# Two middle down projections as seven half-size products each, with scratch tiles divided anew, in a two-layer decoder step

## The chip, the cores and the metric

The kernel runs on one core of a Trainium2 chip, as one launch. The metric is the device time of the launch in microseconds (us), less is better. Engines: PE (TensorE) multiplies, ACT (ScalarE) and DVE (VectorE) work on tiles element by element, POOL (GpSimd) is used here for little but issuing DMAs, SP (SyncE) only issues DMAs.

## The reference

One inference step of a two-layer decoder in float32, for a prompt of 512 tokens and 8 single-token samples, with model width 1024 and feed-forward width 2816. Around each layer's token mixer stand two half layers, each a SwiGLU whose result is halved:

```python
def _swiglu(x, wg, wu, wd):
    return (jax.nn.silu(x @ wg) * (x @ wu)) @ wd
...
x = x + 0.5 * _swiglu(_rmsnorm(x, norm_g[l, 0]), ffn_w_gate[l, 0], ffn_w_up[l, 0], ffn_w_down[l, 0])
...  # pooling mixer in layer 0, sliding-window attention in layer 1
x = x + 0.5 * _swiglu(_rmsnorm(x, norm_g[l, 2]), ffn_w_gate[l, 1], ffn_w_up[l, 1], ffn_w_down[l, 1])
```

So there are four SwiGLUs, called here by `fi` = 0 to 3. They hold nearly all of the products.

## The kernel before

The residual stream lies transposed in SBUF, as eight tiles `x[k]` of 128 features by 520 tokens. Every operand of a product is split into a high and a low float32r part (`xh`/`xl`, `hh`/`hl` for activations, `wh`/`wl` for weights), and a product is three matrix products (`terms`): high by high, low by high, high by low. A matmul covers 128 rows, 128 columns and half of the tokens, 260.

**A half layer** (`ffn`) goes through its 22 blocks of 128 hidden features in three parts, `PARTS = (8, 8, 6)`. For each block a tile makes gate and up products over the eight feature tiles, SiLU and the product of both (`g`), and splits it (`hidden`). After each part its down projection adds into `x`: eight output blocks, each from two pieces of weights, every piece for both halves of the tokens (`mm`, L510 in the profile). The first `NPL[fi]` tiles of a half layer, (4, 3, 2, 3), are plain ones; the others are Strassen tiles (`strassen_tile`; their matmuls are L538): gate and up for both token halves and both halves of the features form a 2 x 2 block product, made from seven products (`product`, 12 matmuls each) instead of eight. For this the activations' sums T1 to T4 are made once per half layer (`sums`), and the weights' sums S1 to S4 for every tile.

**The weights** go through the class `Weights`. Two lists are written in advance: chunks (up to 1 MB, in a ring of three `raw` buffers) and pieces (128 x 512). `W.get` hands out the next piece; `W.prefetch` has `_split` work five pieces ahead: ACT copies the piece to `wh` (L233), DVE subtracts to get `wl` (L234), each in a ring of six. A Strassen chunk has seven pieces, in the order A11, S1, A22 of the chunk before, S2, A12, S4, S3; its own A22 comes after the next chunk's S1. S2 and S4 are made on DVE in the `raw` buffer (L198, L202). S1 and S3 are made by DMA: `loaded` loads the half block once more into a tile `S` (a ring of four), and POOL issues two adding DMAs, into `S` (L192) and into `raw` (L193). Two calls in `_split` set how far this runs ahead, after each piece:

```python
held = any(c < it[0] for c, _, _ in self.items[self.ns + 1 : self.ns + 3])
self.load(it[0] + self.ca - held)
self.add_up(it[0] + 1)
```

`load` issues chunks up to the given one (`ca` is 2), `add_up` calls `loaded` up to the given one. `held` is true where one of the next two pieces is of an earlier chunk.

**The order of the work.** The program is written in one order, and a scheduler in the framework then orders each engine's queue by its own estimates. What goes through `later` keeps the order in which it was written; all loads of weights do so (`ld`, L325, on SP). Each engine takes its queue in order, and so does SP: an issue that waits for a free buffer holds up the issues behind it. PSUM is used as four pairs of banks (`duo`); ACT copies partial results out of it (L618, L620, L623), DVE the rest (L626, L630, L635; in the down projection L688 and L689). Scratch tiles of a half layer come from a pool with two buffers a name, but the name `sb` has four (three in `fi` = 2) of a full tile's size and serves partial sums, the sums T1 to T4 and the down projection's `u`.

Of the kernel before, what the change touches and what calls it, by code (L numbers as in the profile page):

```python
# [11 lines left out]
F32 = mybir.dt.float32  # L12
# [6 lines left out]
P = 128  # L19
# [10 lines left out]

FIRST = 264
NPL = (4, 3, 2, 3)
HD = 64
NB = SP // P
WINS = (2, 4, 8, 16)
# [90 lines left out]
class Weights:  # L126
# [48 lines left out]
                c[2](c[1])  # L175
            self.na += 1

    def sums(self, ch, again):

        G, V, tmp = self.nc.gpsimd, self.nc.vector, {}

        def blk(raw, r, c):
            return rows(raw)[:, r - 1, 4 * c - 4 : 4 * c, :]

        def loaded(raw):
            s1 = self.splp.tile([P, 4, P], F32, tag="S", name="S", bufs=4)
            tmp[1] = s1  # L190
            again(s1)
            G.dma_start(s1, blk(raw, 2, 2), accum_op=ALU.add)  # L192
            G.dma_start(blk(raw, 2, 1), blk(raw, 1, 1), accum_op=ALU.add)  # L193

        self.chunks[ch][2] = loaded

        def s2(raw):
            V.tensor_tensor(blk(raw, 1, 1), blk(raw, 1, 1), tmp[1], op=ALU.add)  # L198
            return blk(raw, 1, 1)

        def s4(raw):
            V.tensor_tensor(blk(raw, 1, 2), blk(raw, 1, 2), blk(raw, 1, 1), op=ALU.add)  # L202
            return blk(raw, 1, 2)

        self.piece(ch, lambda raw: blk(raw, 1, 1))
        self.piece(ch, lambda raw: tmp[1])
        self.last()
        self.piece(ch, s2)
        self.piece(ch, lambda raw: blk(raw, 1, 2))
        self.piece(ch, s4)  # L210
        self.piece(ch, lambda raw: blk(raw, 2, 1))
        self.late = (ch, lambda raw: blk(raw, 2, 2))

    def _split(self, i):
        nc = self.nc
        while self.ns <= min(i, len(self.items) - 1):
            it = self.items[self.ns]
            self.load(it[0])
            self.add_up(it[0])
            src = it[1](self.chunks[it[0]][1])  # L220
            n = src.shape[1]
            if it[2] is not None:
                dh, dl = it[2]()
                wh = wl = None
            else:
                wh = self.splp.tile([P, 4, P], F32R, tag="wh", name="wh")
                wl = self.splp.tile([P, 4, P], F32R, tag="wl", name="wl")
                dh, dl = wh[:, :n, :], wl[:, :n, :]
            if len(src.shape) == 4:
                dh = dh.rearrange("p k (e d) -> p k e d", e=2)  # L230
                dl = dl.rearrange("p k (e d) -> p k e d", e=2)
            pin = self.pin if wh is not None else self.pin_home
            pin(nc.scalar.activation(dh, src, AF.Copy))  # L233
            pin(nc.vector.tensor_tensor(dl, src, dh.bitcast(F32), op=ALU.subtract))  # L234
            it[2] = (wh, wl)
            held = any(c < it[0] for c, _, _ in self.items[self.ns + 1 : self.ns + 3])
            self.load(it[0] + self.ca - held)
            self.add_up(it[0] + 1)
            self.ns += 1

    def get(self):
# [10 lines left out]
def yoco_step(ctx, tc, ins, outs):  # L252
# [21 lines left out]
    def pair(tags, shape, dtype=F32R):  # L274

        return tuple(big.tile(shape, dtype, tag=t, name=t) for t in tags)

    XX, TT, HH = ("xh", "xl"), ("th", "tl"), ("hh", "hl")

    def later(ins):  # L280

        return tc.keep_in_program_order(ins)

    ordered = [False]

    def seq(ins):

        return later(ins) if ordered[0] else ins

    def split(dst, src, scale=None):  # L290

        hi, lo = dst
        if scale is None:
            seq(S.activation(hi, src, AF.Copy))
            seq(V.tensor_tensor(lo, src, hi.bitcast(F32), op=ALU.subtract))
        else:
            seq(S.activation(hi, src, AF.Copy, scale=scale))
            seq(V.scalar_tensor_tensor(lo, src, scale, hi.bitcast(F32), op0=ALU.mult, op1=ALU.subtract))

    ordered = [False]  # L300

# [22 lines left out]
    def ld(dst, src):  # L324
        return lambda raw: later(nc.sync.dma_start(dst(raw), src))  # L325
# [22 lines left out]
    def plan_ffn(l, f):  # L348
        g3 = w_gate[l, f].rearrange("(k p) c -> p k c", p=P)
        u3 = w_up[l, f].rearrange("(k p) c -> p k c", p=P)  # L350
        d3 = w_down[l, f].rearrange("(k p) c -> p k c", p=P)
        t0 = 0
        for n in PARTS:
            for j in range(t0, t0 + n):
                c = slice(j * P, (j + 1) * P)
                cuts = ((0, 4), (4, 8)) if (l, f, j) == (0, 0, 0) else ((0, 8),)
                ch = W.chunk(
                    *[
                        ld(lambda raw, k=k, o=o: rows(raw)[:, o, k[0] : k[1], :], w3[:, k[0] : k[1], c])
                        for k in cuts  # L360
                        for o, w3 in ((0, g3), (1, u3))
                    ]
                )
                if j < NPL[2 * l + f]:
                    for k0 in (0, 4):
                        for o in (0, 1):
                            W.piece(ch, lambda raw, k0=k0, o=o: rows(raw)[:, o, k0 : k0 + 4, :])
                else:
                    W.sums(ch, ld(lambda t: t, u3[:, :4, c]))
            for c in range(4):  # L370
                ch = W.chunk(ld(lambda raw, n=n: raw[:, :n, :], d3[:, t0 : t0 + n, c * 256 : (c + 1) * 256]))
                if (l, f) == (1, 1) and t0 + n == sum(PARTS) and c > 1:
                    if c == 2:
                        plain(ch, n, 0)
                    for k in range(n):
                        W.home(ch, *last_piece(k, c))
                    continue
                plain(ch, n, 0)
                plain(ch, n, P)
            t0 += n  # L380
# [64 lines left out]
    def hcols(t, hf):  # L445
        return t[:, hf * H : (hf + 1) * H]
# [11 lines left out]
            order(V.tensor_tensor(acc[:, :TOK], acc[:, :TOK], sq, op=ALU.add))  # L458

    pss_ = [None]  # L460
    nsb = [4]

    def rstd_tok(tiles=(0, P, 2 * P, 3 * P, 400)):

# [80 lines left out]
                )  # L545

    def hidden(g, hs):
        hp = pair(hs.tags, [P, TOK])
        split(hp, g)
        hs.append(hp)  # L550

    class Hidden(list):


        def __init__(self, tags):
            self.tags = tags

    copied, there = [], [False]

# [46 lines left out]
    def strassen_tile(tmp, xx, tt, hs):  # L606
# [5 lines left out]
        g = tmp.tile([P, TOK], F32, tag="g", name="g")  # L612
        t = tmp.tile([P, TOK], F32, tag="t", name="t")
        sa = tmp.tile([P, TOK], F32, tag="sa", name="sa")
        sb = tmp.tile([P, H], F32, tag="sb", name="sb", bufs=nsb[0])
        a, c = duo()[:, 0, :], duo()
        product(B(xx, lo, 0), a)
        S.copy(hcols(sa, 0), a[:, :H])  # L618
# [18 lines left out]

        unfinished.append(rest)

    def sums(tmp, n, tt):  # L640


        for k in range(4):
            xa = tmp.tile([P, TOK], F32, tag="sa", name="xa")
            xb = tmp.tile([P, TOK], F32, tag="sa", name="xb")
            for kk, xn in ((k, xa), (k + 4, xb)):
                S.activation(xn, x[kk], AF.Copy, scale=gcol(n, kk))
            t12 = tmp.tile([P, TOK], F32, tag="sb", name="t12", bufs=nsb[0])
            t34 = tmp.tile([P, TOK], F32, tag="sb", name="t34", bufs=nsb[0])
            b11, b12, b21, b22 = hcols(xa, 0), hcols(xa, 1), hcols(xb, 0), hcols(xb, 1)  # L650
            t1, t2, t3, t4 = hcols(t12, 0), hcols(t12, 1), hcols(t34, 0), hcols(t34, 1)
            later(V.tensor_tensor(t1, b11, b12, op=ALU.subtract))
            V.scalar_tensor_tensor(t2, t1, -1.0, b22, op0=ALU.mult, op1=ALU.subtract)
            tt[k] = pair(TT, [P, TOK])
            split(tt[k], t12)
            yield
            later(V.tensor_tensor(t3, b22, b12, op=ALU.subtract))
            V.scalar_tensor_tensor(t4, t2, -1.0, b21, op0=ALU.mult, op1=ALU.subtract)
            tt[k + 4] = pair(TT, [P, TOK])
            split(tt[k + 4], t34)  # L660
            yield

    def ffn(fi, tmp, mov, hooks, tt, tags, after, before_last=None, first=None, by_parts=None, hold=False):

        j = 0
        for pi, n in enumerate(PARTS):
            last = pi == len(PARTS) - 1
            hs = Hidden(tags)
            for _ in range(n):
                if j == 0 and first is not None:  # L670
                    plain_end(tmp, *first, hs)
# [5 lines left out]
                    strassen_tile(tmp, mov, tt, hs)  # L677
                j += 1
                W.pin = lambda ins: ins
            nk = (n + 1) // 2  # L680
            rest = NH if last and by_parts is not None else 0

            def add(m, bank, hfs):
                c = slice(hfs[0] * H, (hfs[-1] + 1) * H)
                u = tmp.tile([P, TOK], F32, tag="sb", name="u", bufs=nsb[0])[:, c]
                parts = lambda z: z.rearrange("p (h c) -> p h c", c=H)
                pin = later if last and hold and m == KT - 1 else seq
                pin(V.tensor_tensor(parts(u), bank[:, hfs[0] : hfs[-1] + 1, :H], parts(R[:, c]), op=ALU.mult))  # L688
# [341 lines left out]
        V.tensor_tensor(out, out, sw, op=ALU.add)  # L1030

    mov4 = []
    nsb[0] = 3
    with ff_pool() as tmp:

        s4 = sinks.rearrange("p (g i b e) -> p g i b e", g=2, i=4, b=4)
# [97 lines left out]
        hooks = [step, outputs] + [step] * 4  # L1134
        ffn(2, tmp, mov3, hooks, tt, XX, deferred(4, tmp, "g", HH, mov4), attention_prep())

    nsb[0] = 4

    mov5, mov6 = [], []
    with tc.tile_pool(name="at", bufs=2) as at:  # L1140
# [346 lines left out]
    with ff_pool() as tmp:  # L1487
# [95 lines left out]
        def tail(hs):  # L1583
# [28 lines left out]

            def add(j, bank):
                m = KT - NH + j
                u = tmp.tile([P, TOK], F32, tag="sb", name="u", bufs=nsb[0])[:, c]
                seq(V.tensor_tensor(u, bank, R[:, c], op=ALU.mult))
                seq(V.scalar_tensor_tensor(x[m][:, c], u, -0.5, x[m][:, c], op0=ALU.mult, op1=ALU.add))
                sq = tmp.tile([P, TOK], F32, tag="g", name="sq")
# [110 lines left out]
```

## Time and profile before

| | |
|---|---|
| three runs | 1679.82, 1685.45, 1685.54 us; median 1685.45 us |
| span of the profiled execution, first to last instruction | 1678.4 us |
| PE busy | 1655.2 us (99%) |
| DVE busy | 1241.2 us (74%) |
| ACT busy | 890.0 us (53%) |
| POOL busy | 165.6 us (10%) |
| DMA | 225.97 MB moved, mean 135 GB/s |

The page gives the span of the profiled execution and no total for it; the three runs are 1.4 to 7.1 us longer than that span. Times in the rows below are us from the span's start. A row of a timeline has start, duration, engine, line, operation, output and input, and in brackets how long the engine was idle before and what ended it. SPq is SP issuing a DMA. In the rows of a tile, "DMA to landing" is the time from a DMA's issue to its data being in place.

### The profile page before, as it was taken

To read this page: it belongs to the slowest core of one execution; us is meant where nothing else is said; L and a number is where in the kernel's file an instruction comes from. 1 tells how busy PE (TensorE), PEld (TensorE's weight loads), DVE (VectorE), ACT (ScalarE), POOL (GpSimd) and SP (SyncE) were. 2 spreads that over 40 slices of the span, in tenths; PEclk is the share of its full clock that TensorE was granted. 3 is DMA by queue.
4 is the path that set the end of the run, shared out by engine and by line. 5 is a ranking of instruction groups with operands and counts; after the bars stand their busy time and mean duration, and the time that the engine had idled before them with its cause. 6 is when DMAs were issued, how large, how long until landed. Compare 5 with 4: busy or idle time off the path is not lost.

```text
span 1678.4 us, 34457 instructions
## 1 busy us (share of the span) xinstructions
PE 1655.2 (99%) x13770; PEld 1645.5 (98%) x13770; DVE 1241.2 (74%) x2361; ACT 890.0 (53%) x1768; POOL 165.6 (10%) x224
## 2 busy tenths in 40 slices
PE   9999999999999999999999999999989999999997
PEld 9999999999999999999999999999989999999997
DVE  6866866887975875878775875886787785785776
ACT  5743643666652652655552652655785653463455
POOL 0101101000101101100201101101210100110100
PEclk9999999999999999999999999999999999999999
DMA  8646846652655745643755755653222554674641
GB/s 215 137 122 136 174 140 137 176 161 73 144 145 133 176 145 133 151 132 94 170 148 132 171 151 133 151 149 86 70 51 76 133 136 130 147 173 133 143 127 52
DMA packets 314541, 225.97 MB, mean 135 GB/s; under 512 B 9726, under 2 KB 290022, under 8 KB 314340
## 3 DMA queue, kind: packets, MB, share of 16 engines
q1 hardware_dynamic: 287614, 177.86, 37.6%
q0 software_dynamic: 23008, 40.83, 14.8%
q10 hardware_dynamic: 3758, 5.09, 1.0%
q8 instruction: 108, 1.77, 0.4%
q14 instruction: 53, 0.43, 0.1%
HBM read 180.30 MB, written 5.04 MB: 110 GB/s over the span
## 4 chain that ended last, share of the span: by engine, by line
PE 94%; ACT 2%; DVE 2%; issue 1%; DMA 0%; POOL 0%; ACTq 0%; DVEq 0%; POOLq 0%
PE ps L538 46%; PE ps L510 43%; PE ps L917 1%; PE ps L942 1%; ACT sm L1256 1%; PE ps L1312 1%; ACT xh L310 0%; PE ps L1281 0%; PE ps L1603 0%; PE ps L1610 0%; PE ps L469 0%; ACT oT L1331 0%; PE ps L797 0%; DVE wl L234 0%; PE ps L1224 0%
## 5 line engine op out<-in xcount | busy, mean ns | idle before, releaser
L233 ACT ACTIVATE wh<-raw 128x512 fp32r<-128x512 f32 (+1 forms) x730 | 443.0, 622 | 531.6 <-PE ps L510 315.6
L234 DVE TENSOR_TENSOR wl<-raw,wh 128x512 fp32r<-128x512 f32 (+1 forms) x730 | 483.0, 676 | 209.4 <-ACT wh L233 205.9
L538 PE MATMUL ps<-th,wh 128*128 128x260 f32 x1216 | 343.8, 283 | 0.0
L538 PE MATMUL ps<-tl,wh 128*128 128x260 f32 x1216 | 343.0, 282 | 0.0
L538 PE MATMUL ps<-th,wl 128*128 128x260 f32 x1216 | 341.3, 282 | 0.0
L510 PE MATMUL ps<-hh,wh 128*128 128x260 f32 x1340 | 271.2, 284 | 0.6 <-ACT vtok L1098 0.6
L510 PE MATMUL ps<-hl,wh 128*128 128x260 f32 x1340 | 270.7, 282 | 0.0
L510 PE MATMUL ps<-hh,wl 128*128 128x260 f32 x1340 | 268.5, 282 | 0.0
L538 PEld LDWEIGHTS ps<-tl,wh 128*128 128x128 f32 x1216 | 229.0, 188 | 0.0
L538 PEld LDWEIGHTS ps<-th,wh 128*128 128x128 f32 x1216 | 228.6, 188 | 0.0
L538 PEld LDWEIGHTS ps<-th,wl 128*128 128x128 f32 x1216 | 228.2, 188 | 0.0
L510 PEld LDWEIGHTS ps<-hl,wh 128*128 128x128 f32 x1340 | 207.1, 188 | 0.0
L510 PEld LDWEIGHTS ps<-hh,wh 128*128 128x128 f32 x1340 | 205.5, 188 | 1.5 <-ACT vtok L1098 0.9
L510 PEld LDWEIGHTS ps<-hh,wl 128*128 128x128 f32 x1340 | 205.9, 188 | 0.0
L538 PE MATMUL ps<-xh,wh 128*128 128x260 f32 x672 | 188.2, 283 | 0.0
L538 PE MATMUL ps<-xl,wh 128*128 128x260 f32 x672 | 188.1, 282 | 0.0
L193 POOL DMA_DIRECT2D raw<-raw x76 | 65.6, 864 | 1236.9 <-DVE wl L234 520.8
L538 PE MATMUL ps<-xh,wl 128*128 128x260 f32 x672 | 184.1, 281 | 0.0
L510 PE MATMUL ps<-xl,wh 128*128 128x260 f32 x736 | 149.7, 284 | 0.3 <-DVE xl L816 0.3
L510 PE MATMUL ps<-xh,wh 128*128 128x260 f32 x736 | 149.1, 285 | 0.0
L510 PE MATMUL ps<-xh,wl 128*128 128x260 f32 x736 | 148.0, 283 | 0.0
L688 DVE TENSOR_TENSOR u<-ps,R 128x520 f32<-128x520 f32 x93 | 64.7, 697 | 100.8 <-PE ps L510 100.8
(301 smaller groups left out, 2886.7 us busy)
## 6 DMA issues: line engine op xcount, KB each, us to landing
raw<-in_ffn_w_gate_dram SPq DMA_DIRECT2D x87, 512.0 KB, 4.0
raw<-in_ffn_w_up_dram SPq DMA_DIRECT2D x87, 512.0 KB, 5.4
raw<-in_ffn_w_down_dram SPq DMA_DIRECT2D x32, 1024.0 KB, 5.1
raw<-raw POOLq DMA_DIRECT2D x76, 256.0 KB, 3.3
S<-in_ffn_w_up_dram SPq DMA_DIRECT2D x76, 256.0 KB, 5.6
S<-raw POOLq DMA_DIRECT2D x76, 256.0 KB, 4.6
raw<-in_ffn_w_down_dram SPq DMA_DIRECT2D x16, 768.0 KB, 4.5
raw<-in_w_q_dram SPq DMA_DIRECT2D x8, 512.0 KB, 4.2
```

Of the source, the lines that this page charges most:

```text
L193: G.dma_start(blk(raw, 2, 1), blk(raw, 1, 1), accum_op=ALU.add)
L233: pin(nc.scalar.activation(dh, src, AF.Copy))
L234: pin(nc.vector.tensor_tensor(dl, src, dh.bitcast(F32), op=ALU.subtract))
L510: ins = T.matmul(banks[:, hf, :H], a[:, kk, :], hcols(b, hf), start=(first and i == 0), stop=(last and i == 2),)
L538: T.matmul(bank[:, :H], a[:, kk, :], b, start=(not more and kk == 0 and i == 0), stop=(kk == 3 and i == 2), skip_group_check=more,)
L688: pin(V.tensor_tensor(parts(u), bank[:, hfs[0] : hfs[-1] + 1, :H], parts(R[:, c]), op=ALU.mult))
L917: T.matmul(o, a[:, s], b[:, kk, :], start=(n == 0), stop=(n == 5))
L942: T.matmul(po[:, half * 256 : half * 256 + 256], z[:, tau, c], b, start=(i == 0), stop=(i == len(lst) - 1),)
L1256: S.activation(z, z, AF.Exp, scale=-1.0, bias=nm[:, i : i + 1], accum_out=self.den[:, i : i + 1])
L1312: T.matmul(po[:, bi * 256 : (bi + 1) * 256], a, p_[:, kc_], start=(n == 0), stop=(n == 3 * len(kts) - 1),)
```

## The change

For `fi` = 0 and 1, the second part's down projection (`SEVEN`) becomes a block product of seven half-size products for each pair of output blocks. Rows of the block product are the even and the odd hidden tiles, columns the token halves. Four things come with it.

The hidden tiles are not only split but also summed (`HiddenSums.take`): per pair of tiles T1 to T4 on DVE, and splits of B11, T1 with T2, B21 with B22, and T3 with T4. B11 is put into the right half of the operand tiles `mov[0..3]`, which no Strassen tile reads; the first T3 and T4 take two buffers of the ring `S`. The weights of the down projection are loaded like a Strassen chunk's, with 128 columns a block, and their pieces are woven (`woven`), since the first two pairs of output blocks are begun together. The scratch name `sb` is divided: `sb` has two buffers of half a tile, `u` has two of a full tile. And in `_split` the second call above gets `- held`, which holds for all chunks.

```diff
+SEVEN = {(0, 1), (1, 1)}
...
+    def woven(self, tiles):
+        put = lambda i, *names: [self.piece(tiles[i][0], tiles[i][1][n]) for n in names]
+        put(0, "A11", "S1")
+        self.last()
+        put(1, "A11", "S1")
+        put(0, "S2", "A12", "S4", "S3")
+        put(1, "S2")
+        put(0, "A22")
+        put(1, "A12", "S4", "S3")
+        for i in range(2, len(tiles)):
+            put(i, "A11", "S1")
+            put(i - 1, "A22")
+            put(i, "S2", "A12", "S4", "S3")
+        self.late = (tiles[-1][0], tiles[-1][1]["A22"])
...
             self.load(it[0] + self.ca - held)
-            self.add_up(it[0] + 1)
+            self.add_up(it[0] + 1 - held)
...
+            if (2 * l + f, pi) in SEVEN:
+                tiles = []
+                for m in range(0, KT, 2):
+                    cols = [slice((m + r) * P, (m + r + 1) * P) for r in range(2)]
+                    lo, up = (slice(t0 + o, t0 + n, 2) for o in range(2))
+                    ch = W.chunk(
+                        *[
+                            ld(lambda raw, r=r, o=o: rows(raw)[:, r, o : o + 4, :], d3[:, ks, cols[r]])
+                            for o, ks in ((0, lo), (4, up))
+                            for r in range(2)
+                        ]
+                    )
+                    tiles.append((ch, W.combos(ch, ld(lambda t: t, d3[:, lo, cols[1]]))))
+                W.woven(tiles)
...
+        def take(self, g):
+            k = len(self.b["T3"])
+            if self.even is None:
+                b11 = tuple(hcols(z, 1) for z in self.mov[k])
+                split(b11, hcols(g, 0))
+                self.b["B11"].append(b11)
+                t12 = self.tmp.tile([P, TOK], F32, tag="u", name="t12", bufs=nu[0])
+                t1 = hcols(t12, 0)
+                V.tensor_tensor(t1, hcols(g, 0), hcols(g, 1), op=ALU.subtract)
+                z = pair(self.tags, [P, TOK])
+                self.both(z, "T1", "T2")
+                if 2 * k + 2 == self.n:
+                    split(tuple(hcols(a, 0) for a in z), t1)
+                self.even = g, t12, z
+                return
+            (e, t12, z), self.even = self.even, None
+            t1, t2 = hcols(t12, 0), hcols(t12, 1)
+            t34 = self.tmp.tile([P, TOK], F32, tag="u", name="t34", bufs=nu[0])
+            t3, t4 = hcols(t34, 0), hcols(t34, 1)
+            V.scalar_tensor_tensor(t2, t1, -1.0, hcols(g, 1), op0=ALU.mult, op1=ALU.subtract)
+            if 2 * k + 2 == self.n:
+                split(tuple(hcols(a, 1) for a in z), t2)
+            else:
+                split(z, t12)
+            w = pair(self.tags, [P, TOK])
+            self.both(w, "B21", "B22")
+            split(w, g)
+            V.tensor_tensor(t3, hcols(g, 1), hcols(e, 1), op=ALU.subtract)
+            V.scalar_tensor_tensor(t4, t2, -1.0, hcols(g, 0), op0=ALU.mult, op1=ALU.subtract)
+            v = self.more(k)
+            self.both(v, "T3", "T4")
+            split(v, t34)
...
-        sb = tmp.tile([P, H], F32, tag="sb", name="sb", bufs=nsb[0])
+        sb = tmp.tile([P, H], F32, tag="sb", name="sb", bufs=2)
...
+    def strassen_down(tmp, hs):
+        b, st = hs.b, {}
+        def head(i):
+            a, c = duo()[:, 0, :], duo()
+            sa = tmp.tile([P, TOK], F32, tag="sa", name="sa")
+            sb = tmp.tile([P, H], F32, tag="sb", name="sb", bufs=2)
+            product(b["B11"], a)
+            S.copy(hcols(sa, 0), a[:, :H])
+            product(b["T1"], c[:, 1, :])
+            S.copy(sb, c[:, 1, :H])
+            st[i] = a, c, sa, sb
...
+        head(0)
+        finish()
+        head(1)
+        second(0)
+        third(0)
+        second(1)
+        rest(0)
+        third(1)
+        for i in range(2, KT // 2):
+            head(i)
+            rest(i - 1)
+            second(i)
+            third(i)
+        unfinished.append(lambda: rest(KT // 2 - 1))
...
-            t12 = tmp.tile([P, TOK], F32, tag="sb", name="t12", bufs=nsb[0])
-            t34 = tmp.tile([P, TOK], F32, tag="sb", name="t34", bufs=nsb[0])
+            t12 = tmp.tile([P, TOK], F32, tag="u", name="t12", bufs=nu[0])
+            t34 = tmp.tile([P, TOK], F32, tag="u", name="t34", bufs=nu[0])
...
+            if seven:
+                strassen_down(tmp, hs)
+                continue
```

`second(i)` multiplies T2 with S2, `third(i)` B21 with A12, B22 with S4 and T3 with S3, and `rest(i)` T4 with A22; each ends with the copies and sums that a Strassen tile has, and adds into `x[2 * i]` and `x[2 * i + 1]`.

More of the change, by code (lines that the diff above doesn't have):

```diff
@@ L176, in add_up, with combos @@
             self.na += 1
-    def sums(self, ch, again):
+    def combos(self, ch, again):
         G, V, tmp = self.nc.gpsimd, self.nc.vector, {}
@@ L203, in s4, with sums @@
             return blk(raw, 1, 2)
-        self.piece(ch, lambda raw: blk(raw, 1, 1))
-        self.piece(ch, lambda raw: tmp[1])
-        self.last()
[L208 to L212, printed above, removed]
+        return {
+            "A11": lambda raw: blk(raw, 1, 1),
+            "S1": lambda raw: tmp[1],
+            "S2": s2,
+            "A12": lambda raw: blk(raw, 1, 2),
+            "S4": s4,
+            "S3": lambda raw: blk(raw, 2, 1),
+            "A22": lambda raw: blk(raw, 2, 2),
+        }
+    def sums(self, ch, again):
+        v = self.combos(ch, again)
+        for name in ("A11", "S1"):
+            self.piece(ch, v[name])
+        self.last()
+        for name in ("S2", "A12", "S4", "S3"):
+            self.piece(ch, v[name])
+        self.late = (ch, v["A22"])
+    def woven(self, tiles):
[12 more added lines that the diff above has]
+        self.late = (tiles[-1][0], tiles[-1][1]["A22"])
     def _split(self, i):
@@ L278, in yoco_step @@
     XX, TT, HH = ("xh", "xl"), ("th", "tl"), ("hh", "hl")
[L280 to L298, printed above, removed]
     ordered = [False]
@@ L352, in plan_ffn @@
         t0 = 0
-        for n in PARTS:
+        for pi, n in enumerate(PARTS):
             for j in range(t0, t0 + n):
@@ L369, in plan_ffn @@
                     W.sums(ch, ld(lambda t: t, u3[:, :4, c]))
+            if (2 * l + f, pi) in SEVEN:
[12 more added lines that the diff above has]
+                W.woven(tiles)
+                t0 += n
+                continue
             for c in range(4):
@@ L460, in yoco_step @@
     pss_ = [None]
-    nsb = [4]
+    nu = [2]
     def rstd_tok(tiles=(0, P, 2 * P, 3 * P, 400)):
@@ L547, in hidden @@
     def hidden(g, hs):
-        hp = pair(hs.tags, [P, TOK])
-        split(hp, g)
-        hs.append(hp)
+        hs.take(g)
     class Hidden(list):
@@ L556, in __init__, with both, more, take @@
             self.tags = tags
+        def take(self, g):
+            hp = pair(self.tags, [P, TOK])
+            split(hp, g)
+            self.append(hp)
+    class HiddenSums:
+        def __init__(self, tmp, mov, tags, n):
+            self.tmp, self.mov, self.tags, self.n = tmp, mov, tags, n
+            self.b = {q: [] for q in ("B11", "T1", "T2", "B21", "B22", "T3", "T4")}
+            self.even = None
+        def both(self, z, *names):
+            for hf, q in enumerate(names):
+                self.b[q].append(tuple(hcols(a, hf) for a in z))
+        def more(self, k):
+            if k == 0:
+                return tuple(splp.tile([P, TOK], F32R, tag="S", name=q, bufs=4) for q in ("ph", "pl"))
+            return tuple(self.tmp.tile([P, TOK], F32R, tag=q, name=q, bufs=3) for q in ("ph", "pl"))
+        def take(self, g):
+            k = len(self.b["T3"])
[29 more added lines that the diff above has]
+            split(v, t34)
@@ L638, in strassen_tile, with second, third, rest @@
         unfinished.append(rest)
+    def strassen_down(tmp, hs):
[9 more added lines that the diff above has]
+            st[i] = a, c, sa, sb
+        def second(i):
+            a, c, sa, sb = st[i]
+            product(b["T2"], a, True)
+            S.copy(hcols(sa, 1), a[:, :H])
+        def third(i):
+            a, c, sa, sb = st[i]
+            product(b["B21"], c[:, 0, :])
+            product(b["B22"], c[:, 1, :], True)
+            u = tmp.tile([P, TOK], F32, tag="u", name="u", bufs=nu[0])
+            V.tensor_tensor(halves(u), halves(sa), c[:, :, :H], op=ALU.add)
+            V.tensor_tensor(u, u, R, op=ALU.mult)
+            V.scalar_tensor_tensor(x[2 * i], u, -0.5, x[2 * i], op0=ALU.mult, op1=ALU.add)
+            product(b["T3"], a, True)
+            V.tensor_tensor(sb, sb, a[:, :H], op=ALU.add)
+        def rest(i):
+            a, c, sa, sb = st.pop(i)
+            u = tmp.tile([P, TOK], F32, tag="u", name="u", bufs=nu[0])
+            V.tensor_tensor(hcols(u, 1), sb, hcols(R, 1), op=ALU.mult)
+            product(b["T4"], a, True)
+            V.tensor_tensor(hcols(u, 0), a[:, :H], hcols(R, 0), op=ALU.mult)
+            V.scalar_tensor_tensor(x[2 * i + 1], u, 0.5, x[2 * i + 1], op0=ALU.mult, op1=ALU.add)
+        head(0)
[12 more added lines that the diff above has]
+        unfinished.append(lambda: rest(KT // 2 - 1))
     def sums(tmp, n, tt):
@@ L667, in ffn @@
             last = pi == len(PARTS) - 1
-            hs = Hidden(tags)
+            seven = (fi, pi) in SEVEN
+            hs = HiddenSums(tmp, mov, tags, n) if seven else Hidden(tags)
             for _ in range(n):
@@ L679, in ffn @@
                 W.pin = lambda ins: ins
+            if seven:
+                strassen_down(tmp, hs)
+                continue
             nk = (n + 1) // 2
@@ L684, in add @@
                 c = slice(hfs[0] * H, (hfs[-1] + 1) * H)
-                u = tmp.tile([P, TOK], F32, tag="sb", name="u", bufs=nsb[0])[:, c]
+                u = tmp.tile([P, TOK], F32, tag="u", name="u", bufs=nu[0])[:, c]
                 parts = lambda z: z.rearrange("p (h c) -> p h c", c=H)
@@ L1032, in yoco_step @@
     mov4 = []
-    nsb[0] = 3
     with ff_pool() as tmp:
@@ L1135, in yoco_step @@
         ffn(2, tmp, mov3, hooks, tt, XX, deferred(4, tmp, "g", HH, mov4), attention_prep())
-    nsb[0] = 4
     mov5, mov6 = [], []
@@ L1614, in add @@
                 m = KT - NH + j
-                u = tmp.tile([P, TOK], F32, tag="sb", name="u", bufs=nsb[0])[:, c]
+                u = tmp.tile([P, TOK], F32, tag="u", name="u", bufs=nu[0])[:, c]
                 seq(V.tensor_tensor(u, bank, R[:, c], op=ALU.mult))
```

## The prediction

> **What bounds the kernel now.** I read the head and part 1 of the page, then part 4 (the chain of waits), then the timelines of ACT, DVE, SP and POOL in one steady stretch.
>
> ```profile
> span 1678.4 us, 34457 instructions
> PE 1655.2 (99%) x13770; PEld 1645.5 (98%) x13770; DVE 1241.2 (74%) x2361; ACT 890.0 (53%) x1768; POOL 165.6 (10%) x224
> PE 94%; ACT 2%; DVE 2%; issue 1%; DMA 0%; POOL 0%; ACTq 0%; DVEq 0%; POOLq 0%
> ```
>
> TensorE is busy 99% of the span and is 94% of the chain. So a matmul taken away is worth its full pitch, and whatever makes PE wait is paid in full. What feeds PE is a pipeline: a chunk of weights lands in `raw` (three buffers), a DMA adds S1 into a tile `S`, ACT and DVE split each piece into `wh` and `wl` some five products ahead, PE multiplies. One Strassen tile in the steady state:
>
> ```profile
> 179.62 0.64 ACT L628 ACTIVATE t<-g 128x520 f32<-128x520 f32 x1 [1.37 <-DVE g L627]
> 183.14 0.63 ACT L233 ACTIVATE wh<-S 128x512 fp32r<-128x512 f32 x1 [0.55 <-ACT sb L620]
> 184.59 0.63 ACT L233 ACTIVATE wh<-raw 128x512 fp32r<-128x512 f32 x1 [0.28 <-PE ps L538]
> 189.70 0.64 ACT L628 ACTIVATE t<-g 128x520 f32<-128x520 f32 x1 [1.37 <-DVE g L627]
> 192.31 0.36 ACT L620 COPY sb<-ps 128x260 f32<-128x260 f32 x1
> ```
> ```profile
> 184.16 0.69 DVE L234 TENSOR_TENSOR wl<-S,wh 128x512 fp32r<-128x512 f32 x1
> 185.37 0.68 DVE L234 TENSOR_TENSOR wl<-raw,wh 128x512 fp32r<-128x512 f32 x1
> ```
> ```profile
> 176.00 0.37 SPq L325 DMA_DIRECT2D raw<-in_ffn_w_gate_dram  x1
> 177.46 1.48 SPq L325 DMA_DIRECT2D S<-in_ffn_w_up_dram  x1
> 186.08 0.37 SPq L325 DMA_DIRECT2D raw<-in_ffn_w_gate_dram  x1
> ```
> ```profile
> 183.11 0.86 POOL L193 DMA_DIRECT2D raw<-raw  x1 [8.07 <-DVE wl L234]
> 183.65 1.21 POOL L192 DMA_DIRECT2D S<-raw  x1
> ```
>
> The reader is to see four things. The tile takes 10.08 us (179.62 to 189.70) for 7 products of 12 matmuls, 0.120 us a matmul. S1 is split at 183.14 and at once behind it the previous chunk's last piece, A22, at 184.59; its `wl` ends at 186.05, and at 186.08 SP issues the next chunk's load, which had waited for that buffer. The product that uses the S1 of 183.14 ends just before L620 at 192.31, so it starts near 190.8: S1 (`wl` ready at 184.85) is about 6 us early. And the `S` load of 177.46, whose add is issued on POOL at 183.65, belongs to the chunk loaded with it at 176.00, whose S1 is split only about 17 us after that load. Everything hangs on this spare time.
>
> **The products.** Down pieces now take 24 matmuls each:
>
> ```profile
> 138.42 0.63 ACT L233 ACTIVATE wh<-S 128x512 fp32r<-128x512 f32 x1 [2.25 <-PE ps L510]
> 147.05 0.63 ACT L233 ACTIVATE wh<-raw 128x512 fp32r<-128x512 f32 x1 [2.21 <-PE ps L510]
> ```
>
> These splits are three pieces apart: 8.63 / 72 = 0.120 us a matmul here too. A pair of output blocks has 96 matmuls now and 84 after; four pairs, two middle parts: 96 matmuls fewer (the built programs hold 13,646 and 13,550 matrix instructions). Gain 96 x 0.120 = **-11.5 us**, all on PE.
>
> **The added vector work.** Each pair of hidden tiles gains on DVE one full split (0.69 as above) and five half-width operations, and four pairs of output blocks have seven splits and two sums each.
>
> ```profile
> 180.00:200.00 20.00, 20.00 (x169) 20.00 (x168) 17.26 (x31) 12.36 (x25) 3.50 (x4) 1.00 0.86 184
> L633 DVE TENSOR_TENSOR g<-sb,t 128x260 f32<-128x260 f32 x76 | 32.3, 425 | 4.4
> ```
>
> DVE is busy 17.26 us of 20 in two tiles; 0.69 + 5 x 0.425 = 2.8 more gives 20.1 of the 20.16 that PE takes. That is at the limit but not over it, and ACT (12.36 of 20) has room. I take 0. If that cover is gone and DVE falls 5% behind, it costs 1 us on each of eight pairs of hidden tiles (20.16 us each) and 0.5 us on each of eight pairs of output blocks (10.08 us each): 8 + 4 = 12 us. The start of the new down part has 24 + 9 matmuls (4.0 us) between the last hidden tile's product and the first use of its T2; three half-width operations and a split of 0.4 each are 1.6, so 0, and 1 us each if three `wl` stand ahead. The scratch ring `u` of two is written and read mostly by DVE in its own order: 0, at most a half-width operation at each of 32 sum steps, on DVE and not on PE.
>
> **The moved step.** `add_up(it[0] + 1 - held)` acts in every Strassen tile, 76 of them, not in two parts. `held` is true at A11 and S1 of a chunk, since the previous chunk's A22 follows. So add_up for chunk c+1 moves from A11 of c to S2 of c, three pieces on, and behind `load(c+2)`. In the built program SP's queue read `raw15, S(15), raw16, S(16)` and now reads `raw16, S(15), raw17, S(16)`; POOL's add into `S(15)` now stands behind the L193 add of `raw16`. SP issues in order, and the load of `raw16` waits for A22 of chunk 13. That closes a loop: A22(13) split, raw16 issued, `S(15)` issued and landed, added on POOL and landed, S1(15) split, and right behind it in ACT's and DVE's queues A22(14), which frees the buffer for raw17. Its price comes from where a load follows a pause, at the start of a part:
>
> ```profile
> 154.60 0.63 ACT L233 ACTIVATE wh<-raw 128x512 fp32r<-128x512 f32 x1 [0.79 <-PE ps L538]
> 162.98 0.63 ACT L233 ACTIVATE wh<-S 128x512 fp32r<-128x512 f32 x1
> ```
> ```profile
> 155.99 0.37 SPq L325 DMA_DIRECT2D raw<-in_ffn_w_gate_dram  x1
> 157.03 0.98 SPq L325 DMA_DIRECT2D S<-in_ffn_w_up_dram  x1
> 162.71 1.21 POOL L192 DMA_DIRECT2D S<-raw  x1
> ```
> ```profile
> L192 POOL DMA_DIRECT2D S<-raw x1: 1212/1212/1212, 162.7 to 162.7; - x1
> DMA to landing us min/median/max: 4.4/4.4/4.4
> L192 POOL DMA_DIRECT2D S<-raw x1: 1212/1212/1212, 183.6 to 183.6; - x1
> DMA to landing us min/median/max: 5.0/5.0/5.0
> L325 SPq DMA_DIRECT2D S<-in_ffn_w_up_dram x1: 982/982/982, 157.0 to 157.0; - x1
> DMA to landing us min/median/max: 5.3/5.3/5.3
> L192 POOL DMA_DIRECT2D S<-raw x2: 859/898/937, 142.3 to 143.1; - x2
> DMA to landing us min/median/max: 3.3/3.7/4.0
> ```
>
> From the load's issue to S1 in place: 155.99 to 162.71 + 4.4 = 167.1, 11.1 us after a pause; 176.00 to 183.65 + 5.0 = 188.65, 12.65 us in the steady state, where the chunk before still moves. In the loop the chunk before is done, so I take 11.5, near the first. From S1 in place to the next load's issue: 183.14 to 186.08 is 2.9, with a hidden tile's split between; three DVE operations alone (the S2 sum, `wl` of S1, `wl` of A22) are 2.0; I take 2.3. The loop is **13.8 us against PE's 10.08: 3.7 us a tile**.
>
> That ACT stands still for such a tile, with all behind it, one row shows:
>
> ```profile
> 807.63 0.63 ACT L233 ACTIVATE wh<-S 128x512 fp32r<-128x512 f32 x1 [4.53 <-DMA S<-raw]
> ```
>
> Queued behind S1 are A22, S2 and A12 on ACT, and on DVE the `wl` of these and the next PSUM sums; PE waits for `wh` and `wl`. Splitting ahead can't speed up a loop that runs slower than PE; it only hides the first 6 us of each run of Strassen tiles. The first two chunks of a run keep their order; the third is late by 167.1 - 162.98 = 4.1 us (in the new order its `S` is the one issued at 157.03), each later one by 3.7 more. A run of n tiles so costs 4.1 + 3.7(n - 3) - 6.1: 1.7, 5.4, 9.1 and 16.5 us for n = 4, 5, 6 and 8. Runs end at down parts in plain pieces, which have no S1. The half layers have 4, 8, 6; 5, 8, 6; 6, 8, 6; 5, 8, 6 tiles. In the first two the middle down part is itself made of Strassen chunks, so 8 + 4 + 6 are one run. In its four woven chunks `S` of the second is loaded along with the first's, and A22 of the first stands ten pieces behind its S1, so that two of the steps fit in PE's time; left are 4.1 + 13 x 3.7 - 6.1 = 46.1. Sum: (1.7 + 46.1) + (5.4 + 46.1) + (9.1 + 16.5 + 9.1) + (5.4 + 16.5 + 9.1) = **+165 us**.
>
> **The sum.** The page gives the profiled execution's span, 1678.4, and no total; the three runs are 1.4 to 7.1 us above it, the median 7.05. 1678.4 - 11.5 + 165 = 1832, and with 7.05 around it **1839 us**. Bounds: with the shortest landing seen for each step the loop is 2.0 + 1.04 + 5.3 + 0.4 + 3.3 = 12.0, 2 us a tile and 2.4 late at first, +65 in the same sum, 1739 us. With the steady 12.65 and 2.65 it is 15.3, 5.2 a tile and 5.5 late at first (188.65 - 183.14), +254, 1928 us.
>
> **Rivals.** *The loads land sooner when the queues are empty, and the loop fits into 10.08 us.* Then only the gain is left: 1685.45 - 11.5 = 1674 us, faster. It decides at a load-to-S1 time under 7.8 us; for it speaks that the loop's own pause empties the queues, against it that the row after a pause has 11.1 and the shortest pieces still make 12.0. Chance 0.07. The Trainium skill's page "DMA: Bandwidth & Descriptors", section "Anatomy of one DMA", puts a transfer at about 2.0 us plus its bytes over 436 GB/s; as an estimate that is 5.0 us for chunk and `S` together and 2.6 for the add, and with the 2.3 above a loop of 9.9 us and 1674. The trace doesn't agree: the add of 256 KB took 4.4 and 5.0 us.
>
> *DVE becomes the bound in the two changed parts, and the loop doesn't bind.* The 12 us above against 11.5: 1686 us, no change. For it speaks 20.1 of 20.16; against it that most of DVE's operations overlap at their ends (31 in 17.26 us). Chance 0.04.
>
> *The change doesn't do what it says.* The count of 96 speaks against it, and it isn't given a chance of its own.
>
> **How the numbers follow.** The loop 0.89, faster 0.07, no change 0.04. About 0.5% can be told from no change. All of the loop's cases are slower by more, so slower 0.89, same 0.04, faster 0.07. The range runs between the loop's two bounds, 1739 to 1928; outside are the 0.11 of the rivals and a few hundredths beyond either bound.
>
> **What would show it.** On the timeline of after: in steady stretches, also of the third and fourth half layer, which the products don't touch, L628's successor some 13 to 14 us apart instead of 10.08; ACT `wh<-S` with idle time ahead of it ended by "DMA S<-raw", some 3.7 us a tile; PE's busy share near 90%, its idle time ended by `wh` or `wl`. Wrong it is if `wh<-S` comes without a wait in these stretches, or if the slowdown lies only in the two changed parts (then DVE or the woven order is the cause). The size is wrong if the landing of `S<-raw` leaves 3.3 to 5.1 us.

## The result, and the profile after

The changed kernel takes 1846.75 us (median of four runs, 1845.01 to 1848.84) against 1682.63 us (four runs, 1677.90 to 1685.54): ratio 1.0988, 95% interval 1.0962 to 1.1015. Forecast were 1839 us and a range of 1739 to 1928. The head of its page, part 1, the first line of part 4 and two lines of part 6 (KB each, median us from issue to landing):

```profile
span 1843.2 us, 34524 instructions
PE 1712.9 (93%) x13674; PEld 1672.4 (91%) x13674; DVE 1281.9 (70%) x2475; ACT 895.3 (49%) x1834; POOL 179.9 (10%) x240
...
PE 25%; DVE 6%; DMA 5%; issue 3%; ACT 2%; POOL 0%; SPq 0%; DVEq 0%; ACTq 0%; POOLq 0%
...
S<-raw POOLq DMA_DIRECT2D x84, 256.0 KB, 4.2
S<-in_ffn_w_up_dram SPq DMA_DIRECT2D x76, 256.0 KB, 5.6
```

PE has 96 matmuls fewer (13770 to 13674), as counted. But the chain that ended last is no longer PE's. The profile follows it back only to 1047.5 us, so its shares add up to 41% of the span; of these 41, PE has 25 (before, 94 of 99), and DVE and DMAs are on it. PE's idle time went from 23.2 to 130.3 us. It is also busy 57.7 us longer although it does less. Its mean granted clock was 0.975 against 0.994; as an estimate, (1655.2 - 11.5) x (0.994 / 0.975 - 1) = 32 us come from that, and what the rest is stays open.

What the engines waited for, over the whole span (us in total, times, longest):

```profile
ACT wh L258 <- DMA S<-raw: 247.6, 64, 7.5
DVE raw L196 <- DMA S<-raw: 145.0, 51, 5.7
POOL S L190 <- DMA S<-in_ffn_w_up_dram: 131.5, 20, 13.5
ACT t L702 <- DVE g L701: 123.9, 52, 4.3
...
PEld ps L559 <- ACT wh L258: 81.8, 71, 3.4
```

L258 is the split that was L233, L559 are the Strassen matmuls that were L538, L190 and L191 are the POOL adds that were L192 and L193, L196 is the S2 sum that was L198, L702 the ACT operation on a hidden tile that was L628, and L330 (below) the SP load that was L325. The splits of S1 wait 64 times for POOL's add, 3.9 us each. One run of tiles in the first half layer, from the timelines of ACT and of SP:

```profile
154.88 0.63 ACT L258 ACTIVATE wh<-S 128x512 fp32r<-128x512 f32 x1 [0.55 <-ACT sa L692]
169.03 0.63 ACT L258 ACTIVATE wh<-S 128x512 fp32r<-128x512 f32 x1 [3.64 <-DMA S<-raw]
182.67 0.64 ACT L258 ACTIVATE wh<-S 128x512 fp32r<-128x512 f32 x1 [3.42 <-DMA S<-raw]
196.18 0.63 ACT L258 ACTIVATE wh<-S 128x512 fp32r<-128x512 f32 x1 [3.57 <-DMA S<-raw]
211.00 0.63 ACT L258 ACTIVATE wh<-S 128x512 fp32r<-128x512 f32 x1 [5.69 <-DMA S<-raw]
```
```profile
185.22 0.37 SPq L330 DMA_DIRECT2D raw<-in_ffn_w_gate_dram  x1
185.63 0.58 SPq L330 DMA_DIRECT2D raw<-in_ffn_w_up_dram  x1
186.25 0.82 SPq L330 DMA_DIRECT2D S<-in_ffn_w_up_dram  x1
198.77 0.37 SPq L330 DMA_DIRECT2D raw<-in_ffn_w_gate_dram  x1
```

The tiles are 13.64, 13.51 and 14.82 us apart in place of 10.08. The loop can be walked in two steps: raw's load issued at 185.22, `S` right behind it, S1 split at 196.18 (10.96 us); A22's split lets the next load go at 198.77 (2.59 us): 13.55 together. PE's share in the same place, in windows (length; busy us and matmuls of PE, then PEld, DVE, ACT, POOL; granted clock; DMA share; GB/s):

```profile
180.00:200.00 20.00, 16.41 (x128) 15.40 (x127) 13.81 (x25) 8.81 (x18) 1.75 (x2) 1.00 0.52 113
200.00:220.00 20.00, 16.98 (x128) 16.55 (x128) 15.67 (x30) 10.13 (x21) 2.58 (x4) 0.91 0.65 157
```

128 matmuls stand where before had 169. DVE was busy 17.26 us there before and is 13.81 now, so it isn't the bound.

### The profile page after: what moved, and what is told of

It is laid out like the page before. It is cut to its first block, busy times and chain, and to the rows that moved or that the text cites. A ratio compares the mean times of both kernels' runs of the same rounds, so it can differ in the third digit from the quotient of the medians.

```text
span 1843.2 us, 34524 instructions
## 1 busy us (share of the span) xinstructions
PE 1712.9 (93%) x13674; PEld 1672.4 (91%) x13674; DVE 1281.9 (70%) x2475; ACT 895.3 (49%) x1834; POOL 179.9 (10%) x240
## 5 line engine op out<-in xcount | busy, mean ns | idle before, releaser
L258 ACT ACTIVATE wh<-raw 128x512 fp32r<-128x512 f32 (+1 forms) x746 | 433.6, 615 | 354.0 <-PE ps L531 246.7
L559 PE MATMUL ps<-th,wh 128*128 128x260 f32 x1216 | 362.9, 299 | 78.1 <-ACT wh L258 48.3
L559 PE MATMUL ps<-th,wl 128*128 128x260 f32 x1216 | 357.3, 297 | 16.3 <-DVE wl L259 15.4
L559 PE MATMUL ps<-tl,wh 128*128 128x260 f32 x1216 | 354.3, 292 | 0.0
L559 PEld LDWEIGHTS ps<-th,wh 128*128 128x128 f32 x1216 | 241.1, 198 | 93.3 <-ACT wh L258 65.1
L559 PEld LDWEIGHTS ps<-th,wl 128*128 128x128 f32 x1216 | 239.6, 198 | 26.8 <-DVE wl L259 26.5
L559 PEld LDWEIGHTS ps<-tl,wh 128*128 128x128 f32 x1216 | 241.3, 198 | 0.0
L531 PE MATMUL ps<-hh,wh 128*128 128x260 f32 x1084 | 219.1, 284 | 0.6 <-ACT vtok L1228 0.6
L531 PE MATMUL ps<-hl,wh 128*128 128x260 f32 x1084 | 218.1, 282 | 0.0
L531 PE MATMUL ps<-hh,wl 128*128 128x260 f32 x1084 | 217.6, 282 | 0.0
L559 PE MATMUL ps<-xh,wh 128*128 128x260 f32 x704 | 198.9, 284 | 2.0 <-ACT wh L258 2.0
L559 PE MATMUL ps<-xl,wh 128*128 128x260 f32 x704 | 198.3, 283 | 0.0
L559 PE MATMUL ps<-xh,wl 128*128 128x260 f32 x704 | 197.7, 282 | 0.0
L191 POOL DMA_DIRECT2D raw<-raw x84 | 72.6, 865 | 1273.2 <-DVE wl L259 423.2
L196 DVE TENSOR_TENSOR raw<-raw,S 128x512 f32<-128x512 f32 x84 | 58.1, 692 | 189.2 <-DMA S<-raw 145.0
L258 ACT ACTIVATE wh<-S 128x512 fp32r<-128x512 f32 x84 | 53.0, 631 | 267.5 <-DMA S<-raw 247.6
L531 PEld LDWEIGHTS ps<-hh,wh 128*128 128x128 f32 x1084 | 166.5, 189 | 1.5 <-ACT vtok L1228 0.9
L531 PEld LDWEIGHTS ps<-hl,wh 128*128 128x128 f32 x1084 | 167.1, 188 | 0.0
L531 PEld LDWEIGHTS ps<-hh,wl 128*128 128x128 f32 x1084 | 167.0, 188 | 0.0
```

Of the source, the lines that this page charges most:

```text
L531: ins = T.matmul(banks[:, hf, :H], a[:, kk, :], hcols(b, hf), start=(first and i == 0), stop=(last and i == 2),)
L559: T.matmul(bank[:, :H], a[:, kk, :], b, start=(not more and kk == 0 and i == 0), stop=(kk == 3 and i == 2), skip_group_check=more,)
```

## The experiments

**The one line in the kernel before.** Everything of the change is left out but this:

```
-            self.add_up(it[0] + 1)
+            self.add_up(it[0] + 1 - held)
```

> The kernel before with one edit, add_up(it[0] + 1 - held); all down projections stay in plain pieces. Loop theory (the S load stands behind the next chunk's load): runs of 4, 8, 6; 5, 8, 6; 6, 8, 6; 5, 8, 6 tiles, each 4.1 + 3.7(n - 3) - 6.1, is 27.3 + 31.0 + 34.7 + 31.0 = 124 us, so about 1807 us (1790 to 1825), slower. Rival, the vector work and the woven order of the two changed parts: no change, 1683 us.

Measured: 1817.05 us against 1678.41 (ratio 1.0821, interval 1.0805 to 1.0837). Its waits and timeline show the same loop:

```profile
ACT wh L233 <- DMA S<-raw: 216.5, 53, 7.2
```
```profile
170.57 0.64 ACT L233 ACTIVATE wh<-S 128x512 fp32r<-128x512 f32 x1 [3.76 <-DMA S<-raw]
183.94 0.63 ACT L233 ACTIVATE wh<-S 128x512 fp32r<-128x512 f32 x1 [3.24 <-DMA S<-raw]
197.64 0.63 ACT L233 ACTIVATE wh<-S 128x512 fp32r<-128x512 f32 x1 [4.13 <-DMA S<-raw]
```

So 139 us come from one line that has nothing to do with the down projection.

**The same delay, the other order on SP.** `held` moves two things: `S(c+1)`'s load is asked for three pieces later, and it stands behind raw(c+2)'s load. Here only the first is kept:

```
-            self.load(it[0] + self.ca - held)
-            self.add_up(it[0] + 1)
+            self.add_up(it[0] + 1 - held)
+            self.load(it[0] + self.ca - held)
```

> The same edit, and the two calls change places, so that add_up, still three pieces later than before, stands ahead of load. Loop theory: S is issued right behind its own chunk again, nothing closes a loop, 1683 us within 0.5%. Rival, that add_up is called three pieces later whatever the queue's order: as slow as the kernel without the exchange, about 1807 us.

Measured: 1681.92 us (ratio 1.0025, 1.0013 to 1.0037).

```profile
ACT wh L233 <- DMA S<-raw: 3.8, 2, 2.5
```
```profile
182.93 0.63 ACT L233 ACTIVATE wh<-S 128x512 fp32r<-128x512 f32 x1 [0.55 <-ACT sb L620]
192.99 0.63 ACT L233 ACTIVATE wh<-S 128x512 fp32r<-128x512 f32 x1 [0.53 <-ACT sb L620]
203.05 0.63 ACT L233 ACTIVATE wh<-S 128x512 fp32r<-128x512 f32 x1 [0.53 <-ACT sb L620]
```

53 waits became 2, and the tiles are 10.06 us apart. The lateness by three pieces costs next to nothing (0.25%); the place behind a load that waits for a buffer costs 135 us.

The place has two sides, and this run does not tell them apart. POOL takes its adds in order too, and in the kernel with the one line the add into `S` (L192) stands behind the L193 add of the next chunk, which waits for that chunk's load to land. SP's rows, then POOL's:

```profile
214.50 0.58 SPq L325 DMA_DIRECT2D raw<-in_ffn_w_up_dram  x1
215.12 1.23 SPq L325 DMA_DIRECT2D S<-in_ffn_w_up_dram  x1
```
```profile
220.55 0.86 POOL L193 DMA_DIRECT2D raw<-raw  x1 [12.79 <-DMA raw<-in_ffn_w_up_dram]
221.35 0.95 POOL L192 DMA_DIRECT2D S<-raw  x1
```

The exchange puts `S` back beside its own chunk on both queues (in its trace, SP issues the two at 175.79 and 177.31, POOL their adds at 183.41 and 183.94, and S1 is split at 192.99). That the order closes the loop is shown; whether POOL's order alone would do it was not tested.

**The changed kernel without the loop, in both ways.** All of the change, but once with `add_up(it[0] + 1)` as before, and once with `- held` and `add_up` placed ahead of `load`, as just shown.

> The changed kernel with add_up(it[0] + 1) as before, all else changed. Loop theory: only the 96 products are left, 1682.6 - 11.5 = 1671 us (up to 1683 if DVE falls 5% behind in the two parts). Rival, vector work and woven order: near 1847 us.

> The changed kernel with add_up(it[0] + 1 - held) ahead of load. Loop theory: 1671 us, as with add_up of before, up to 1683 if DVE falls behind. Rival, add_up three pieces later: near 1847 us.

Measured: 1678.07 us (ratio 0.9992, 0.9983 to 1.0002) and 1675.59 us (0.9982, 0.9965 to 0.9998). The loop's price in the changed kernel is then, from the ratios, (1.0988 - 0.9982) x 1678.41 = 169 us. But of the 11.5 us that the removed matmuls were reckoned to be worth, the medians show only 0.3 and 2.8 (the second's interval reaches to 5.9). The second of these has the lowest median of all kernels here, 0.2% below the kernel before; its interval overlaps the first's.

**Where the gain went: the parts of the change one by one.** Queue order as before in all three; `SEVEN` empty, or one of its two entries:

```
-SEVEN = {(0, 1), (1, 1)}
+SEVEN = set()      # then {(0, 1)}, then {(1, 1)}
```

> The kernel after with no middle part formed from seven products (all eight-product form again) and the second load queued as in the kernel before: what is left of the change is the new division of the scratch tiles. With the loop gone, both changed parts together should have saved 96 matmuls x 0.120 = 11.5 us and 0 to 3 us were measured. Theory A (the parts give the gain back themselves: short stalls at their ends, and a lower granted clock): this kernel is level with the kernel before, 1678 within 3 us. Theory B (the ring of two for the scratch tiles delays work everywhere and eats the gain): 8 to 10 us slower, 1686 to 1689.

> As the kernel after with the second load queued as in the kernel before, but only the first half layer's middle part in seven products. 48 matmuls fewer, 5.8 us at full value. Theory A: the part's own stalls in the trace with both parts were about 0.25 + 1.3 us, so 3 to 5 us faster than the kernel before at the same granted clock, 1674 to 1676, less where the clock is lower. Theory B (scratch): 8 to 10 us lost and 5.8 won, 1681 to 1683.

> The same with only the second half layer's middle part in seven products. Its stalls in the trace with both parts were about 0.4 + 0.25 us, so theory A: 5 us faster than the kernel before at the same granted clock, 1673 to 1675. Theory B: 1681 to 1683. If the two parts' gains do not add up to that of both (0 to 3 us measured), something that only both together bring is open.

Measured against 1677.95 us: 1679.07 (ratio 1.0011, 1.0002 to 1.0020), 1677.07 (0.9999, 0.9990 to 1.0008) and 1677.20 (0.9993, 0.9984 to 1.0002). The scratch tiles cost 1.8 us, not 8 to 10, so theory B falls. Each part then saves about 2 us of its 5.8 (1679.07 to 1677.07 and 1677.20), less than theory A named for an equal clock. Two things in the traces go the right way. One is short pauses of PE. In the kernel with both parts and the old queue order, PE's busy time by windows is no longer full at the new down parts' starts and ends:

```profile
220.00:240.00 20.00, 19.75 (x162) 19.34 (x162) 18.64 (x37) 13.03 (x28) 3.44 (x4) 1.00 0.71 171
300.00:320.00 20.00, 18.73 (x154) 18.34 (x153) 14.74 (x27) 10.84 (x22) 1.72 (x2) 1.00 0.81 194
440.00:460.00 20.00, 19.61 (x162) 19.19 (x161) 16.55 (x29) 11.51 (x23) 1.73 (x2) 1.00 0.46 95
600.00:620.00 20.00, 19.76 (x162) 19.34 (x161) 18.76 (x36) 12.89 (x27) 2.95 (x4) 1.00 0.68 156
620.00:640.00 20.00, 20.00 (x170) 20.00 (x169) 19.73 (x37) 10.54 (x22) 3.44 (x4) 1.00 0.77 193
```

The first four rows lose 2.2 us in all, of which the third row's 0.4 also appears with the scratch tiles alone. In the attention stage (1140 to 1260) PE idles 8.6 us against 7.0 before, and 8.5 with the scratch tiles alone; so these 1.6 us and the 0.4 would account for the scratch tiles' 1.8. The other is the clock. Over the runs, the mean granted clock was 0.994 before and 0.992 and 0.993 in the two kernels without the loop; with one part it was 0.9935 and 0.9925 against 0.9947. A thousandth of 1660 us of PE work is 1.7 us. Together, 2.2 + 1.6 + about 1.5 to 3 us of clock leave some 5 to 6 of the 11.5. The medians show 0.3 and 2.8, so some 3 to 5 us stay open. Runs of equal granted clock point the same way: at 0.995 the four runs of the kernel with `add_up` ahead of `load` have a mean of 1673.2 us and the eight of the kernel before 1678.3, 5 us apart where the medians show 2.8. So, by these runs, a part of the gain is there and is covered by a lower clock.

**Is the price per late tile, or does it feed on itself?** In the kernel before, with the one line only in every second tile, and only in two of three:

```
-            self.add_up(it[0] + 1)
+            self.add_up(it[0] + 1 - (held and it[0] % 2))        # or: it[0] % 3 > 0
```

> The kernel before with the one-line change, but only in every second tile: there S(c+1)'s load stands behind raw(c+2)'s on SP, in the tiles between it is asked for early as before. With it in all tiles the time was 1817, 139 us more. Loop theory: the lateness feeds on itself only from one late tile to the next; a single late tile is 4.1 us late against a run-ahead of 6.1 us, and the tile after it is on time and lets the run-ahead be made up again: 1678 to 1690. Rival (each late tile costs its 3.7 us by itself, wherever it stands): half of the 139 us, 1748.

> The same in two of every three tiles. Loop theory: two late tiles in a row are 4.1 + 3.7 us late against a run-ahead of 6.1, 1.7 us for each group, some 20 groups, if the run-ahead is full again each time: 1700 to 1725, more where one tile on time doesn't refill it. Rival (a fixed price for each late tile): two thirds of the 139 us, 1771.

Measured: 1743.73 us (ratio 1.0390, 1.0374 to 1.0405) and 1755.35 us (1.0454, 1.0436 to 1.0473) against 1678.15. My reading of the loop failed here: a tile on time does not let the run-ahead be made up. The waits of the two kernels, in that order:

```profile
ACT wh L233 <- DMA S<-raw: 101.5, 25, 7.0
```
```profile
ACT wh L233 <- DMA S<-raw: 123.0, 37, 5.6
```

65.6 us over 25 waits, 77.2 over 37 and, with the line in all tiles, 138.6 over 53: 2.6, 2.1 and 2.6 us for each late tile. The rival, a fixed price, fits the first of the two kernels (1748 named) and is 16 us too high for the second (1771 named); why a late tile costs less there stays open. SP's and ACT's timelines of the first show what one tile on time does:

```profile
178.91 0.37 SPq L325 DMA_DIRECT2D raw<-in_ffn_w_gate_dram  x1
...
192.29 0.37 SPq L325 DMA_DIRECT2D raw<-in_ffn_w_gate_dram  x1
...
201.05 0.37 SPq L325 DMA_DIRECT2D raw<-in_ffn_w_gate_dram  x1
...
202.10 2.90 SPq L325 DMA_DIRECT2D S<-in_ffn_w_up_dram  x2
```
```profile
190.30 0.63 ACT L233 ACTIVATE wh<-S 128x512 fp32r<-128x512 f32 x1 [3.70 <-DMA S<-raw]
...
197.54 0.63 ACT L233 ACTIVATE wh<-S 128x512 fp32r<-128x512 f32 x1
...
213.43 0.63 ACT L233 ACTIVATE wh<-S 128x512 fp32r<-128x512 f32 x1 [4.67 <-DMA S<-raw]
```

The late tile takes 13.38 us from load to load (178.91 to 192.29), the one on time 8.76 (192.29 to 201.05). It takes back 1.3 of the 3.3 us over 10.08; why not more was not tested. Then `S` is late again: 190.30 to 213.43 is 23.1 us for two tiles against 20.16. As these rows read, the loop closes over two tiles as well as over one.

## Why the prediction was right, point by point

- **What bounds.** Half right. With PE at 99%, waits put into its feed lengthened the run by 139 us in the kernel with the one line alone. The other half of that sentence, that a matmul taken away is worth its full pitch, did not come out (see the products).
- **The moved step.** Right in place and mechanism, and near in size. The one line alone makes +139 us, the order of the two calls decides it, and the loop has 10.96 + 2.59 = 13.55 us in the quoted tile where 11.5 + 2.3 = 13.8 was taken. The sum was +165; the runs give 169. The landing of `S<-raw` has a median of 4.2 us, inside the 3.3 to 5.1 named.
- **The run-ahead.** The sum let the first 6.1 us of each run of tiles be hidden. For whole runs that roughly works: the same terms give +124 for the kernel before with the line alone, 139 were measured. The step from there to the changed kernel, with its woven parts, was 41 us in the sum (165 - 124) and is 30 in the runs (169 - 139). The two misses partly cancel, so that 165 came so near to 169 is in part luck. The idea that I built on it for the tests, that one punctual tile restores the run-ahead, was wrong.
- **The products.** The count was right, the worth wrong: -11.5 us were summed, the changed kernels without the loop are 0.3 and 2.8 us below the kernel before in their medians. This is the term that failed; beside 165 it hardly showed in the total. In all, +153.6 us were forecast (1839 against 1685.45) and +164.1 measured (1846.75 against 1682.63); the gain that did not come is about the size of this difference of 10.5 us.
- **Added vector work, start of the part, scratch.** Taken as 0. The pauses above are 2.2 us and the scratch tiles 1.8. The DVE rival, 12 us, is not what happened: in the busiest of the quoted rows, 620 to 640, DVE is at 19.73 us of 20 and PE loses nothing; in the next, at 18.76, it loses 0.24 us.
- **The signs.** `wh<-S` waits with 3.4 to 5.7 us of idle time where 3.7 was named; PE is at 93% of the span where 90% was named for the steady stretches (82% in the quoted window, 16.41 of 20). The same intervals appear where no product is changed, in the third half layer:

```profile
1053.67 0.63 ACT L258 ACTIVATE wh<-S 128x512 fp32r<-128x512 f32 x1 [4.86 <-DMA S<-raw]
1067.28 0.63 ACT L258 ACTIVATE wh<-S 128x512 fp32r<-128x512 f32 x1 [4.09 <-DMA S<-raw]
1080.79 0.63 ACT L258 ACTIVATE wh<-S 128x512 fp32r<-128x512 f32 x1 [4.39 <-DMA S<-raw]
```

- **The rival of short landings** needed a load-to-S1 time under 7.8 us; 10.96 were measured. By the figures that the prediction took from the Trainium skill's page "DMA: Bandwidth & Descriptors", section "Anatomy of one DMA", the add alone is, as an estimate, 2.6 us; here its median is 4.2 us with the DMA engines about half busy (0.52 in the quoted window), so the trace does not agree. That section of the Trainium skill gives these figures for DMAs issued by GpSimd: that covers the add, and not SP's loads, for which the prediction used them too.

## What to carry to other kernels

When a change moves a DMA past another in an in-order queue, ask what the other one waits for: if that is a buffer freed by work that needs the moved DMA, the two close a loop, and where it is longer than the bottleneck's turn, its length, not any engine, sets the pace. Walk the loop step by step on the timeline and compare it with the bottleneck's time for one turn. And look at a small line in shared code before the large new function: it acts in every tile.

## What was not expected of the hardware

In some windows in which PE pauses or has just paused, the granted clock is lower, and the price of a pause is then more than its length. Windows in the attention stage (the number behind POOL's is the granted clock): the kernel before, then the changed kernel with `add_up` ahead of `load`:

```profile
1230.00:1240.00 10.00, 7.97 (x64) 7.11 (x61) 8.40 (x27) 9.75 (x31) 2.51 (x3) 0.83 0.02 5
1250.00:1260.00 10.00, 10.00 (x74) 9.83 (x74) 6.92 (x28) 5.30 (x22) 1.89 (x2) 0.85 0.48 106
```
```profile
1230.00:1240.00 10.00, 6.58 (x59) 5.74 (x59) 8.77 (x31) 9.38 (x30) 3.44 (x4) 0.96 0.48 106
1240.00:1250.00 10.00, 10.00 (x53) 9.55 (x51) 5.02 (x17) 3.95 (x13) 1.30 (x2) 0.50 0.01 2
1250.00:1260.00 10.00, 10.00 (x62) 10.00 (x63) 6.25 (x27) 5.42 (x21) 1.89 (x2) 0.69 0.48 106
```

PE is busy for all of the second kernel's last two windows, at 0.50 and 0.69 of its clock: by an estimate from these, 5.0 + 3.1 = 8 us of work lost behind 3.4 us of pause. In other windows a pause leaves the clock at 1.00, as in the changed kernel's 180 to 200 above, where PE idles 3.6 us. The longest single wait of PE in this stage of the kernel before, from the waits of 1140 to 1260, is this one (in the second kernel 1.8):

```profile
PE ps L1369 <- ACT oT L1331: 1.5, 1, 1.5
```

The Trainium skill's page "TensorE: Matmul & The Clock Gate", section "Part 1: The HAM clock gate (the "warmup" mystery)", says that the clock is halved after an idle window of about 3.4 us and full again after a busy one of that length. As an estimate from that page of the Trainium skill, one halved window in 10 us is a mean of 1 - 0.5 x 0.34 = 0.83, and the 0.83 above agrees with it, as does 0.50 for a stretch halved throughout. Two things here do not follow from these figures of the Trainium skill: the clock falls in a stage whose single pauses are 1.5 to 1.8 us at most, and in the second kernel it stays down through unbroken matmuls for all of one window and, at 0.69, for some 6.2 us of the next (an estimate), where the Trainium skill's page has it full again after about 3.4 us. The run in this trace took 1683.52 us, at a mean clock of 0.990; the runs of the same kernel with a mean clock of 0.995 took 1672.4 to 1674.0. Where the clock falls differs from trace to trace, and what sets it was not tested; it may hide part of the 3 to 5 us left open.
